# Storing the inverse row sums of a softmax from their column form

## The chip, the cores and the metric

The kernel runs on one core of a Trainium2 chip. A core has a matrix engine (TensorE, PE in the profile; its weight loads are shown apart as PEld), a vector engine (VectorE, DVE), an engine for activations (ScalarE, ACT), a general one (GpSimd, POOL) and one that issues transfers (SyncE, SP), each with an instruction queue that it works through in order. Sixteen DMA engines move data between device memory (DRAM) and the on-chip memory SBUF. TensorE writes into eight banks of an accumulation memory (PSUM). The metric is the time of one execution on the device, in microseconds (us).

## The reference

One layer of a decoder over 1024 tokens of width 1024, in float32. A combined projection gives a pooled branch (four groups of 128 channels) and eight attention heads of width 64 with a forget gate. Attention is causal, with a bias from the running sum of the gates' logarithms:

```python
s = einsum('bhqd,bhkd->bhqk', qb, k) * scale
s = s + cq[..., :, None] - cf[..., None, :]
s = where(kpos <= qpos, s, NEG_INF)
p = softmax(s, axis=-1)
out = einsum('bhqk,bhkd->bhqd', p, v)
...
x = layer_norm(ALPHA * x + concat(pool_out, attn_out) @ w_out)
x = layer_norm(ALPHA * x + square(relu(x @ w_mlp1)) @ w_mlp2)
```

The MLP's hidden width is 4096. The part in question is the division in the softmax: each of the 8 × 1024 rows of `p` has one sum, by whose inverse the row's 64 outputs are multiplied.

## The kernel before

Every float32 matrix product is done as three products of a high and a low part (`three`, L80 to L84). The stages follow one another on TensorE: the projection of values and gates, the pooled groups, attention for four pairs of heads, the output projection with the first normalization, and then the MLP's two products in a form that needs fewer multiplications (L796, L1136). All is one instruction stream; a scheduler orders each engine's queue by its own estimates, so an edit at one place can shift instructions for some distance around it.

Attention works in units: a pair of heads `p`, one head `e` of the pair, and a block `m` of 256 queries. The first three pairs run `m` from 3 down to 0, head by head; the last pair runs `m` from 0 up to 3 with both heads at each `m`. While one unit's probabilities are made, the unit before it is multiplied with its values, and pieces of other work (the next pair's query and key projection, in the last pair one pooled group and the output projection) are put in between by a credit counter (`fillstep`).

- `att_probs` (L353 to L383) makes the unit's probabilities for two rows of 128 queries. TensorE writes logits to a bank `s` (L375), DVE adds the bias and takes a minimum (L380), and ACT takes the exponential (L382), whose sum over the keys it adds up into one column of `rsum[h]`, a tile of 128 queries by 8 query rows.
- `att_values` (L385) turns the probabilities with TensorE into one of two banks named `pt` (L405), ACT and DVE copy them out as a high and a low part (L406, L407), and TensorE multiplies them with the values into a bank `pv` (L420). The two halves are added into a tile `U` (L429, L430), which SP stores to `mix_dram` (L432, L434). So the attention output is stored with the channels in partitions and the queries along the row, undivided.
- The inverses are taken by DVE in `att_values` (L443) from `rsum[h]`: for the first three pairs once a head, at `m == 0`, all eight columns; in the last pair for each unit, two columns. They stand as columns, 128 queries in the partitions. `row_scales` (L463 to L469) runs behind the unit's last multiplication: TensorE turns the columns into rows of a `pt` bank (L466), ACT copies these rows to a tile `row` (L468), and SP stores them to `rin_dram`, 8 heads by 1024 queries (L469). There are 14 such calls.
- `attention_part` (L577 to L586) reads `mix_dram` and, spread over 64 partitions for each head, the rows of `rin_dram` (L580), multiplies them on DVE (L584), and splits the product for the output projection (`out_proj`), whose weights come partly from `wo_dram` (L561).

The names in the profile's rows are those of these tiles; numbers behind a name are left out there.

Of the kernel before, what the change touches and what calls it, by code (L numbers as in the profile page):

```python
# [14 lines left out]
P = 128  # L15
S = 1024
D = 1024
NT = S // P
# [18 lines left out]
def trunk(ctx, tc, xT, xn, wuqk, wvf, bf, poolw, pscale, wout, g1, b1, w1, w2, g2, b2, out):  # L37
# [5 lines left out]
    nc = tc.nc  # L43
# [7 lines left out]
    def slot(tag, shape, dt=F32R):  # L51
        uid[0] += 1
        return sb.tile([P] + list(shape), dt, tag=tag, bufs=NBUF[tag], name=f"{tag}{uid[0]}")

    def small(shape, tag, dt=F32, bufs=1, pool=None):
        uid[0] += 1
        return (pool or sb).tile(list(shape), dt, tag=tag, bufs=bufs, name=f"{tag}_{uid[0]}")
# [5 lines left out]
    def bank(tag=None):  # L63
        uid[0] += 1
        if tag is None:
            tag = CYCLE[rr[0] % 8]
            rr[0] += 1
        return ps.tile([P, CH], F32, tag=tag, bufs=PBUF[tag], name=f"{tag}{uid[0]}")
# [18 lines left out]
    ident = small([P, P], "ident")  # L87
# [17 lines left out]
    rin_dram = dr.tile([NH, S], F32, name="rin_dram")  # L105
# [152 lines left out]
    def run(gen):  # L258
        for _ in gen:
            pass  # L260
# [124 lines left out]
    def att_values(p, e, m, prob, ahead):  # L385
        h = 2 * p + e
        rows = slice(e * HD, (e + 1) * HD)
        orow = slice((1 - e) * HD, (2 - e) * HD)
        if "values" not in fill:
            fill["values"] = bank("pv")  # L390
        ov = fill["values"][:, 256 * fill["half"] : 256 * fill["half"] + 256]
        fill["half"] = 1 - fill["half"]

        def turned(jp):
            tp = bank("pt")
            tt = slot("A", [2, CH])
            if jp < m:
                blocks = [(jj * 256 + ii * P, 2 * jp + jj, ii) for jj in range(2) for ii in range(2)]
                ev = slice(0, CH)
            else:  # L400
                blocks = [(P, 2 * jp + 1, 1), (2 * P, 2 * jp, 0), (3 * P, 2 * jp, 1)]
                ev = slice(P, CH)
                nc.gpsimd.memset(tt[:, :, 0:P].bitcast(F32), 0.0)
            for col, j, ii in blocks:
                fill["turn"] = nc.tensor.transpose(tp[:, col : col + P], prob[ii][:, j * P : (j + 1) * P], ident).ins  # L405
            nc.scalar.copy(tt[:, 0, ev], tp[:, ev])  # L406
            fill["sub"] = nc.vector.tensor_tensor(tt[:, 1, ev], tp[:, ev], tt[:, 0, ev].bitcast(F32), ALU.subtract).ins  # L407
            return tt

        def multiply(jp, tt):  # L410
            mov = ((0, 256), (256, CH)) if jp < m else ((256, CH), (0, 256))
            with ExitStack() as order:
                for behind in (fill["piece"], fill["turn"]):
                    if behind:
                        order.enter_context(tc.issue_after(behind))
                for s in range(2):
                    for jj in range(2):
                        j = 2 * jp + jj
                        a, b = mov[jj]
                        nc.tensor.matmul(  # L420
                            ov, V[j][:, h].rearrange("p s d -> p (s d)"), tt[:, s, a:b],
                            start=(j == 0 and s == 0), stop=(j == 2 * m + 1 and s == 1),
                        )
            if jp == m:
                last = p == NPAIR - 1
                if not last or e == 0:
                    fill["mx"] = slot("U", [256], F32)
                mx = fill["mx"]
                nc.scalar.copy(mx[rows], ov[orow])  # L429
                nc.vector.tensor_tensor(mx[rows], ov[rows], mx[rows], ALU.add)  # L430
                if not last:
                    nc.sync.dma_start(mix_dram[m, rows, NG + p, :], mx[rows])  # L432
                elif e:
                    nc.sync.dma_start(mix_dram[m, :, NG + p, :], mx)  # L434
                if last:
                    row_scales(h, 2 * m, 2)
                elif m == 0:
                    row_scales(h, 0, NT)

        if p == NPAIR - 1 or m == 0:  # L440
            ri = small([P, NT], "ri", bufs=3)
            i, n = (2 * m, 2) if p == NPAIR - 1 else (0, NT)
            nc.vector.reciprocal(ri[:, :n], rsum[h][:, i : i + n])  # L443
            inverse[h, i] = ri

        for jp in range(m + 1):
            left.append((multiply, jp, turned(jp)))
            if jp == 0:
                fill["last"] = fill["sub"]
                next(ahead, None)  # L450
            if jp == min(m, (m + 1) // 2 + 1):
                run(ahead)
            fillstep()
            values(2)

    left, inverse = [], {}

    def values(n):
        while len(left) > n:
            step, jp, tt = left.pop(0)  # L460
            step(jp, tt)

    def row_scales(h, i, n):  # L463
        ri = inverse.pop((h, i))
        tp = bank("pt")
        nc.tensor.transpose(tp[0:n, 0:P], ri[:, :n], ident)  # L466
        row = small([NT, P], "row")
        nc.scalar.copy(row[0:n], tp[0:n, 0:P])  # L468
        nc.sync.dma_start(rin_dram[h, i * P : (i + n) * P].rearrange("(i q) -> i q", q=P), row[0:n])  # L469

    g0 = qk_proj(0)
    for _ in range(2 * KT):
# [222 lines left out]
    def fillstep():  # L695
        fill["credit"] += fill["rate"]
        while fill["credit"] >= 1.0:
            fill["credit"] -= 1.0
            piece = next(fill["gen"], None)
            if piece and fill["pieces"] < 8:  # L700
                fill["piece"], fill["pieces"] = piece, fill["pieces"] + 1
# [4 lines left out]
    for n, unit in enumerate(order):  # L706
        p = n // 8
        if n % 8 == 0:
            if p + 1 < NPAIR:
                gen, pieces, over = qk_proj(p + 1, "mm"), 4 * KT + 1, 28  # L710
            else:
                gen, pieces, over = last_fill(), 2 * KT + 2 + 4 * KT, 27
            fill.update(gen=gen, credit=0.0, rate=pieces / over)
        prob = {}
        ahead = att_probs(*unit, prob)
        if pend is None:
            run(ahead)
        if n + 1 < len(order):
            gate_row(2 * order[n + 1][0] + order[n + 1][1])
        if pend is None:  # L720
            for g in EARLY[1:]:
                pool_linear(g, "A")
        fillstep()
        if pend is not None:
            att_values(*pend, ahead)
        pend = (*unit, prob)
        if n % 8 == 7 and n + 1 < len(order):
            run(gen)
    att_values(*pend, iter(()))
    values(0)  # L730
    run(gen)
# [603 lines left out]
```

## Time and profile before

| | |
|---|---|
| median of 3 runs | 1028.21 us (1027.87 to 1028.32) |
| the profiled execution | 1028.26 us, its span 1026.5 us |
| granted TensorE clock in it | 0.997 of full speed |
| busy: PE, PEld, DVE, ACT, POOL | 99%, 82%, 73%, 50%, 15% of the span |
| first and last reciprocal (L443) | 134.2 and 322.8 us |
| first and last transpose of inverses (L466) | 143.3 and 329.9 us |
| packets, data moved | 113399 packets, 206.17 MB |

The profile is of one execution and its times are counted from the start of the span. In a group's row stand the line, the engine, the operation and the tiles written and read, then the count, the busy time and the mean of one, and behind a bar the idle time before them with what ended most of it. In a row of the timeline the first two numbers are start and duration, and in square brackets stands the idle time before it and what ended it. Matmuls overlap, so a row's duration is longer than the distance to the next start.

### The profile page before, as it was taken

What the parts mean: (1) busy time and instruction counts of PE and PEld (TensorE: products, weight loads), DVE (VectorE), ACT (ScalarE), POOL (GpSimd) and SP (SyncE); (2) the same over time, 40 slices, a digit from 0 to 9 for tenths busy, and PEclk for the clock granted to TensorE, in tenths of its full rate; (3) what the DMA queues carried; (4) which work ended last, traced back from release to release, by engine and by line L of the source; (5) the groups of instructions that cost most, each with busy time, mean ns of one, the idle gap of its engine ahead of it and who ended that gap; (6) DMA issues with size and microseconds to landing.
All of it is one profiled execution on the core that took longest, in us unless ns stands there. A gap on an engine that the chain in (4) does not pass through costs nothing.

```text
span 1026.5 us, 14095 instructions
## 1 busy us (share of the span) xinstructions
PE 1013.1 (99%) x4976; PEld 843.8 (82%) x4976; DVE 754.4 (73%) x1303; ACT 513.3 (50%) x825; POOL 153.6 (15%) x269
## 2 busy tenths in 40 slices
PE   9999999999999999999999999999999999999996
PEld 9988888888788888888888888888888888888884
DVE  6576677777868798989888787798866565565547
ACT  5423665666755333678667667669521121221152
POOL 0200111111110032112221221220000000000057
PEclk9999999999999999999999999999999999999998
DMA  9702211111682633259676675665999888878753
GB/s 354 285 28 88 97 52 53 34 48 52 205 290 91 188 141 103 82 185 362 235 273 236 241 275 222 251 260 191 350 309 289 298 265 264 289 237 274 231 179 123
DMA packets 113399, 206.17 MB, mean 201 GB/s; under 512 B 9576, under 2 KB 77608, under 8 KB 113328
## 3 DMA queue, kind: packets, MB, share of 16 engines
q1 hardware_dynamic: 94176, 136.97, 40.7%
q0 software_dynamic: 18720, 67.64, 17.0%
q8 instruction: 39, 0.64, 0.2%
q10 hardware_dynamic: 432, 0.66, 0.2%
q14 instruction: 32, 0.26, 0.1%
HBM read 132.29 MB, written 72.94 MB: 200 GB/s over the span
## 4 chain that ended last, share of the span: by engine, by line
PE 58%; DVE 2%; issue 0%; ACT 0%; DVEq 0%
PE s L1136 17%; PE s L796 11%; PE pv L1136 9%; PE mm L796 7%; PE pt L796 7%; PE pv L796 4%; PE pt L1136 2%; PE mm L1136 2%; DVE B L71 0%; DVE bns L639 0%; DVE A L664 0%; DVE pt L661 0%; DVE pt L1153 0%; DVE A L870 0%; DVE pv L1153 0%
## 5 line engine op out<-in xcount | busy, mean ns | idle before, releaser
L71 ACT CAST B<-S 128x1024 fp32r<-128x1024 f32 (+1 forms) x78 | 67.6, 880 | 162.9 <-DMA S<-in_w_dram 85.0
L796 PE MATMUL s<-B,Q 128*128 128x512 f32 x492 | 116.4, 389 | 0.2 <-ACT B L71 0.2
L796 PEld LDWEIGHTS s<-B,Q 128*128 128x128 f32 x492 | 92.3, 188 | 19.7 <-ACT B L71 0.6
L71 DVE TENSOR_TENSOR B<-S,B 128x1024 fp32r<-128x1024 f32 (+1 forms) x78 | 78.0, 1008 | 37.7 <-ACT B L71 37.6
L1136 PE MATMUL s<-B,Q 128*128 128x512 f32 x402 | 98.5, 390 | 0.0
L1136 PEld LDWEIGHTS s<-B,Q 128*128 128x128 f32 x402 | 75.5, 188 | 16.5
L71 ACT CAST Q<-S 128x1024 fp32r<-128x1024 f32 (+2 forms) x54 | 55.7, 1031 | 63.6 <-PE s L796 17.0
L921 POOL DMA_DIRECT2D hid_dram<-A x90 | 48.1, 538 | 218.1 <-ACT A L918 171.5
L1136 PE MATMUL s<-B,A 128*128 128x512 f32 x321 | 80.3, 394 | 0.0
L71 DVE TENSOR_TENSOR Q<-S,Q 128x1024 fp32r<-128x1024 f32 (+2 forms) x54 | 65.5, 1213 | 12.8 <-ACT Q L71 12.6
L796 PE MATMUL pt<-B,Q 128*128 128x512 f32 x312 | 74.6, 389 | 0.0
L1136 PEld LDWEIGHTS s<-B,A 128*128 128x128 f32 x321 | 60.4, 188 | 13.9
L796 PE MATMUL mm<-B,Q 128*128 128x512 f32 x300 | 71.6, 389 | 0.0
L382 ACT ACTIVATE A<-A,nm 128x1024 f32<-128x1024 f32 (+7 forms) x64 | 49.7, 777 | 42.0 <-DVE nm L380 41.9
L407 DVE TENSOR_TENSOR A<-pt,A 128x512 fp32r<-128x512 f32 (+1 forms) x80 | 50.1, 633 | 25.1 <-ACT A L406 24.3
L796 PEld LDWEIGHTS pt<-B,Q 128*128 128x128 f32 x312 | 58.5, 188 | 12.1
L796 PEld LDWEIGHTS mm<-B,Q 128*128 128x128 f32 x300 | 56.3, 188 | 11.7
L919 DVE TENSOR_TENSOR A<-A,A 128x1024 f32<-128x1024 f32 x45 | 53.6, 1218 | 0.0
L406 ACT CAST A<-pt 128x512 fp32r<-128x512 f32 (+1 forms) x80 | 42.4, 541 | 22.2 <-PE pt L405 21.6
L375 PE MATMUL s<-Q,Q 128*128 128x512 f32 (+2 forms) x192 | 52.2, 368 | 1.3 <-DVE nm L380 1.3
L420 PE MATMUL pv<-A,B 128*128 128x256 f32 x320 | 53.1, 289 | 0.2 <-DVE U L430 0.2
L420 PEld LDWEIGHTS pv<-A,B 128*128 128x128 f32 x320 | 45.8, 189 | 6.4 <-DVE U L430 3.2
(432 smaller groups left out, 2290.1 us busy)
## 6 DMA issues: line engine op xcount, KB each, us to landing
hid_dram<-A POOLq DMA_DIRECT2D x105, 512.0 KB, 3.8
S<-in_w_dram SPq DMA_DIRECT2D x62, 512.0 KB, 4.4
Q<-hid_dram SPq DMA_DIRECT2D x98, 256.0 KB, 5.3
A<-hid_dram SPq DMA_DIRECT2D x82, 256.0 KB, 5.3
S<-in_wuqk_dram SPq DMA_DIRECT2D x12, 512.0 KB, 4.7
wo_dram<-Q POOLq DMA_DIRECT2D x10, 512.0 KB, 4.3
B<-wo_dram SPq DMA_DIRECT2D x10, 512.0 KB, 6.8
Q<-hid_dram SPq DMA_DIRECT2D x39, 128.0 KB, 3.2
```

The source lines that it names most:

```text
L71: return nc.scalar.copy(hi, src).ins, nc.vector.tensor_tensor(lo, src, hi.bitcast(F32), ALU.subtract).ins
L375: nc.tensor.matmul(sp, rows, KS[:, a:b], start=n == 0, stop=n == 1 and not diag)
L382: nc.scalar.activation(pt[:, :nk], pt[:, :nk], AF.Exp, bias=nm, scale=-1.0, accum_out=rsum[h][:, i : i + 1])
L406: nc.scalar.copy(tt[:, 0, ev], tp[:, ev])
L407: fill["sub"] = nc.vector.tensor_tensor(tt[:, 1, ev], tp[:, ev], tt[:, 0, ev].bitcast(F32), ALU.subtract).ins
L420: nc.tensor.matmul(ov, V[j][:, h].rearrange("p s d -> p (s d)"), tt[:, s, a:b], start=(j == 0 and s == 0), stop=(j == 2 * m + 1 and s == 1),)
L796: nc.tensor.matmul(dst, b[x][:, k], A[a][y][:, k], start=first and k == 0 and i == 0, stop=k == H - 1 and i == 2, skip_group_check=not first,)
L919: nc.vector.tensor_tensor(x, x, hi.bitcast(F32), ALU.subtract)
L921: nc.gpsimd.dma_start(hid_dram[self.u, :, i, AT[name] : AT[name] + 2 * CH], part.rearrange("p q n t -> p (q n t)"))
L1136: nc.tensor.matmul(dst, h[:, p_], w[q_], start=first and u == self.us[0] and j == 0, stop=u == self.us[-1] and j == 2, skip_group_check=no ...
```

## The change

The inverses are stored where they are made. `ri` goes from SBUF straight to `rin_dram`, one float at a time: the store's pattern takes the 128 partitions as the fast index of the row in memory and the two or eight columns as the slow one. The transpose, the copy and the store of rows are gone, and with them `row_scales` and its tile; `ri` has four buffers in place of three, as a store now reads it. The values in `rin_dram` and its readers are the same.

```diff
@@ -432,16 +432,12 @@
                     nc.sync.dma_start(mix_dram[m, rows, NG + p, :], mx[rows])
                 elif e:
                     nc.sync.dma_start(mix_dram[m, :, NG + p, :], mx)
-                if last:
-                    row_scales(h, 2 * m, 2)
-                elif m == 0:
-                    row_scales(h, 0, NT)
 
         if p == NPAIR - 1 or m == 0:
-            ri = small([P, NT], "ri", bufs=3)
             i, n = (2 * m, 2) if p == NPAIR - 1 else (0, NT)
+            ri = small([P, NT], "ri", bufs=4)
             nc.vector.reciprocal(ri[:, :n], rsum[h][:, i : i + n])
-            inverse[h, i] = ri
+            nc.sync.dma_start(rin_dram[h, i * P : (i + n) * P].rearrange("(i q) -> q i", q=P), ri[:, :n])
 
...
-    left, inverse = [], {}
+    left = []
 
...
-    def row_scales(h, i, n):
-        ri = inverse.pop((h, i))
-        tp = bank("pt")
-        nc.tensor.transpose(tp[0:n, 0:P], ri[:, :n], ident)
-        row = small([NT, P], "row")
-        nc.scalar.copy(row[0:n], tp[0:n, 0:P])
-        nc.sync.dma_start(rin_dram[h, i * P : (i + n) * P].rearrange("(i q) -> i q", q=P), row[0:n])
```

TensorE's queue is quoted where the first head's inverses were turned. `A` are the probabilities, `mm` the projection that is threaded in, `pv` the product with the values; the numbers tell the buffers apart. Before:

```order
L82 MATMUL mm_1478<-B_404,B_1475 128x512
L466 MATMUL pt_1543<-ident_63,ri_1433 8x128
L83 MATMUL mm_1478<-B_404,B_1475 128x512
L84 MATMUL mm_1478<-B_404,B_1475 128x512
L405 MATMUL pt_1548<-ident_63,A_1457 128x128
L405 MATMUL pt_1548<-ident_63,A_1444 128x128
L420 MATMUL pv_1216<-A_1436,B_417 128x256 x4
L405 MATMUL pt_1548<-ident_63,A_1457 128x128
L405 MATMUL pt_1548<-ident_63,A_1444 128x128
```

And now:

```order
L82 MATMUL mm_1479<-B_404,B_1476 128x512
L405 MATMUL pt_1544<-ident_63,A_1458 128x128
L405 MATMUL pt_1544<-ident_63,A_1445 128x128
L405 MATMUL pt_1544<-ident_63,A_1458 128x128
L405 MATMUL pt_1544<-ident_63,A_1445 128x128
L83 MATMUL mm_1479<-B_404,B_1476 128x512
L84 MATMUL mm_1479<-B_404,B_1476 128x512
L420 MATMUL pv_1216<-A_1437,B_417 128x256 x4
```

The four value transposes took the place, and the bank, of the transpose of the inverses, ahead of two projection matmuls; they are no longer parted by the four value matmuls.

The second place is SP's queue at the begin of the last pair, where loads of the output weights (`wo_dram`) are issued. Before:

```order
L561 DMA B_3065<-wo_dram 128x1024
L561 DMA B_3066<-wo_dram 128x1024
L432 DMA mix_dram<-U_3041 64x256
L561 DMA B_3215<-wo_dram 128x1024
L469 DMA rin_dram<-row_3120 8x128
L561 DMA B_3216<-wo_dram 128x1024
L432 DMA mix_dram<-U_3114 64x256
```

And now:

```order
L549 DMA B_3047<-wo_dram 128x1024
L440 DMA rin_dram<-ri_2986 128x2x1
L440 DMA rin_dram<-ri_3060 128x2x1
L549 DMA B_3048<-wo_dram 128x1024
L432 DMA mix_dram<-U_3023 64x256
L549 DMA B_3184<-wo_dram 128x1024
L549 DMA B_3185<-wo_dram 128x1024
L432 DMA mix_dram<-U_3097 64x256
L440 DMA rin_dram<-ri_3104 128x2x1
```

The store of a head's eight columns moved up out of this stretch, and the last pair's first two stores came in between the first load and the second. All lines behind the edit count 4 or 12 fewer than before (the reads of `rin_dram` are L568, the loads of `wo_dram` L549).

## The prediction

> **What bounds the kernel now.** I read the page first, then the busy time by stage, then the stage of the change by tile, by wait and row by row. The page:
>
> ```profile
> PE 1013.1 (99%) x4976; PEld 843.8 (82%) x4976; DVE 754.4 (73%) x1303; ACT 513.3 (50%) x825; POOL 153.6 (15%) x269
> PE   9999999999999999999999999999999999999996
> PEclk9999999999999999999999999999999999999998
> PE 58%; DVE 2%; issue 0%; ACT 0%; DVEq 0%
> ```
>
> TensorE is busy in every slice at its full clock, and the chain that ended last lies on it. The busy share alone could hide stalls, so the stages (columns: stage, its length, busy time and instructions of PE, PEld, DVE, ACT, POOL, clock, share of the DMA engines, GB/s):
>
> ```profile
> 125.00:345.00 220.00, 217.84 (x1270) 181.17 (x1269) 164.99 (x395) 137.76 (x295) 33.11 (x85) 1.00 0.34 107
> 275.00:300.00 25.00, 24.73 (x143) 20.22 (x142) 16.87 (x43) 15.79 (x38) 3.50 (x7) 1.00 0.88 295
> 345.00:1026.00 681.00, 671.55 (x2969) 552.07 (x2967) 508.17 (x735) 319.94 (x433) 110.90 (x144) 1.00 0.68 236
> ```
>
> The change lies in 125 to 345 us, attention and the work threaded through it. There DVE is busy for 165 and ACT for 138 of 220 us: TensorE is the bound, but it takes part in chains with both. After 345 us come the MLP's matmuls, 2969 of them in 681 us, 0.23 us each; that stage follows whatever time TensorE comes out of attention, so a microsecond saved on TensorE's queue before 345 should arrive at the end as one. In 275 to 300 us the DMA engines are 88% busy, which matters below for the stores.
>
> **What is removed.** Fourteen of each (six with eight columns, eight with two), from the views by tile of `ri` and of `row` (minimum, median, maximum in ns; first and last start):
>
> ```profile
> L443 DVE RECIPROCAL ri<-rsum x14: 154/166/203, 134.2 to 322.8; 128x2 f32<-128x2 f32 x8, 128x8 f32<-128x8 f32 x6
> L466 PE MATMUL pt<-ident,ri x14: 270/272/275, 143.3 to 329.9; 128*2 128x128 f32 x8, 128*8 128x128 f32 x6
> L468 ACT COPY row<-pt x14: 237/254/255, 143.6 to 330.3; 2x128 f32<-2x128 f32 x8, 8x128 f32<-8x128 f32 x6
> L469 SPq DMA_DIRECT2D rin_dram<-row x14: 244/264/295, 143.9 to 330.6; - x14
> ```
>
> The reciprocals stay. The transpose's 272 ns is latency, not what it costs the queue, for matmuls overlap. The timeline of TensorE around the first one (start, duration) shows the queue's cost:
>
> ```profile
> 142.85 0.40 PE L84 MATMUL mm<-B,B 128*128 128x512 f32 x1
> 143.08 0.40 PE L82 MATMUL mm<-B,B 128*128 128x512 f32 x1
> 143.31 0.27 PE L466 MATMUL pt<-ident,ri 128*8 128x128 f32 x1
> 143.34 0.47 PE L83 MATMUL mm<-B,B 128*128 128x512 f32 x1
> 143.66 0.40 PE L84 MATMUL mm<-B,B 128*128 128x512 f32 x1
> ```
>
> Undisturbed, one 512-column matmul starts 0.23 us after the other (142.85, 143.08). From 143.08 to 143.66 stand two such steps, 0.46 us, and the transpose: 0.58 − 0.46 = 0.12 us. Fourteen of them: 14 × 0.12 = 1.7 us of TensorE's queue, surely gone.
>
> Then the waits. `row` is copied out of a `pt` bank, of which there are two, and the value transposes (L405) use the same two. They wait for the copy (us in total, times), and the transpose itself waits for the bank:
>
> ```profile
>   PEld pt L405: 2.3, 6
>   PE pt L405: 0.3, 1
> PEld pt L466 <- DVE A L407: 1.4, 6, 0.2
> ```
>
> One such wait in the row-by-row view:
>
> ```profile
> 275.47 0.33 PE L375 MATMUL s<-Q,Q 128*128 128x384 f32 x1
> 276.07 0.66 PE L405 MATMUL pt<-ident,A 128*128 128x128 f32 x4 [0.27 <-ACT row L468]
> 276.48 0.42 PE L375 MATMUL s<-Q,Q 128*128 128x384 f32 x1
> 276.75 0.23 PE L377 MATMUL s<-maskb,identb 128*128 128x128 bf16 x1
> ```
>
> The 384-column matmul at 275.47 holds the queue 0.60 us to the next start; its twin at 276.48 needs 0.27. So 0.33 us are really lost at this place. Weight loads run ahead of the matmuls by about one load, which is why 2.3 us of waiting there is not 2.3 us of TensorE: I take off one load of 0.19 us (188 ns in the page's groups, row below) per wait, 2.3 − 6 × 0.19 = 1.2 us, the 0.3 us being part of it. Bounds of this term: 0.3 us (what the matmul queue itself shows as idle) and 2.6 us (both rows in full). The 1.4 us before L466 I count as nothing: the next transposes ask for the same bank, freed by the same DVE subtraction, so that wait passes to them; at most 1.4 − 6 × 0.19 = 0.3 us.
>
> ```profile
> L796 PEld LDWEIGHTS s<-B,Q 128*128 128x128 f32 x492 | 92.3, 188 | 19.7 <-ACT B L71 0.6
> ```
>
> ACT loses 14 × 0.254 = 3.6 us of 138. It is not the bound, and I count zero; but ACT is in order, and what follows the copy there is the exponential of the next unit, for which transposes wait:
>
> ```profile
> PEld s L375 <- DVE nm L380: 4.2, 9, 0.9
> PEld pv L420 <- DVE U L430: 3.2, 10, 0.6
> PEld pt L405 <- ACT A L382: 2.2, 8, 0.4
> ```
>
> The third row, 2.2 us, is the upper bound of a gain there. The first two are the stalls that the change doesn't touch and that could swallow what it saves.
>
> **What is added and moved.** No instruction is new on TensorE, DVE or ACT. The fourth `ri` buffer costs nothing in time: a reciprocal waits only for a store four units back. New is the store's shape: 128 × 8 or 128 × 2 single floats 4 bytes each, set down 512 bytes apart along a partition's elements, instead of 8 or 2 rows of 512 bytes. Nothing in the trace is stored like this, so I bound it. Issuing: a row store takes 0.26 us on SP's queue, a broadcast read of `rin_dram` with more pieces 0.60 us (median):
>
> ```profile
> L580 SPq DMA_DIRECT2D S<-rin_dram x10: 477/597/654, 281.3 to 350.3; - x10
> ```
>
> If issuing grew with the pieces, the 1024 pieces of an early store would hold SP for some microseconds, but SP has room there: around the first store it issues a load and the store 2.2 us apart and sits in between,
>
> ```profile
> 141.71 0.33 SPq L75 DMA_DIRECT2D S<-in_wuqk_dram  x1
> 143.90 0.29 SPq L469 DMA_DIRECT2D rin_dram<-row  x1
> ```
>
> and no wait of TensorE for a DMA stands in the list of waits of this stage. Transfer: between 309 and 312 us there are 378 packets, nearly all of 1 KB, on one queue:
>
> ```profile
> q1 hardware_dynamic: 378, 0.36, 48.4%
> ```
>
> 48.4% of 16 × 3 us is 23.2 us, 61 ns a packet. A 4-byte packet costs between nothing and this; an early store then is 64 packets on each engine, 0 to 3.9 us, a late one 16, 0 to 1.0 us. I take the low end, as 4 bytes are far below 1 KB, and keep the high one for the slow rival.
>
> The place on SP: the store now stands behind the reciprocal instead of behind the row's copy, so what is queued behind it waits for DVE. The tightest spot is where two late stores stand between two loads of `wo_dram`:
>
> ```profile
> 269.18 0.16 DVE L443 RECIPROCAL ri<-rsum 128x2 f32<-128x2 f32 x1
> 272.55 0.17 DVE L443 RECIPROCAL ri<-rsum 128x2 f32<-128x2 f32 x1
> 267.28 1.56 SPq L561 DMA_DIRECT2D B<-wo_dram  x2
> 273.10 0.53 SPq L561 DMA_DIRECT2D B<-wo_dram  x1
> 284.81 2.31 SPq L561 DMA_DIRECT2D B<-wo_dram  x5
> B<-wo_dram SPq DMA_DIRECT2D x10, 512.0 KB, 6.8
> 281.94 0.39 PE L82 MATMUL mm<-B,Q 128*128 128x512 f32 x1
> 295.85 0.41 PE L82 MATMUL mm<-B,Q 128*128 128x512 f32 x1
> ```
>
> The second load of the first row, issued by 268.8 before, now waits for the reciprocal at 272.55: 4 us late, landing near 272.55 + 6.8 = 279.4. Its matmuls are the fourth triple of the output projection, which begins at 281.94, so not before 281.94 + 9 × 0.23 = 284.0: covered by 4.6 us; without that cover the 4 us would be TensorE's. The last five loads land by 287.1 + 6.8 = 293.9; the attention half's first matmul that can need them starts at 295.85. Cover: 2 us.
>
> **Sum.** −1.7 (slots) − 1.2 (bank waits) + 0 (ACT, SP, DMA) = −2.9 us against the profiled execution's 1028.26 (span 1026.5, 1.8 outside it, untouched): 1025.4. The median of the runs, 1028.21, is 0.05 beside it, so the same number stands. Its own range, by the bounds of the bank term and the 0.3: −1.7 − 0.3 to −1.7 − 2.6 − 0.3, that is 1023.7 to 1026.3. The finishing parts after attention (the reads of `mix_dram` and `rin_dram`, the multiplication, the split) move with TensorE or have room.
>
> **Rivals.**
>
> *The waits move on.* The matmul slots saved are spent waiting for DVE: 4.2 and 3.2 us already stand there, and the new order puts transposes directly behind one another where L466 and two matmuls stood between. For it: these waits have nothing to do with `row`. Against it: there is matmul work to fill in from the projection. Half of the slots' 1.7 us survives: about 1027.4.
>
> *More than the sum.* Exponentials come earlier by the copy that stood before them, and the 2.2 us on ACT goes too, with the bank waits in full: 1.7 + 2.6 + 2.2 = 6.5, 1021.8. For it: the copy stands directly before L382 at the first place. Against it: ACT is idle a third of this stage.
>
> *Slower, by the single-float stores.* They share the queue with the `wo_dram` loads where DMA is 88% busy. One early store and four late ones fall between 261 and 293 us: 64 + 4 × 16 = 128 packets an engine. At 61 ns these are 7.8 us; less 2 us cover, TensorE waits 5.8 us, less the 2.9 saved: +2.9, 1031.2. It turns slower above (2 + 2.9) / 128 = 38 ns a packet.
>
> The Trainium skill speaks for this rival: "DMA: Bandwidth & Descriptors", section "Rules for kernel authors", says that a strided last dimension becomes one descriptor per element and is to be rearranged instead. The same page's "Specifications" has it that below 512 bytes the engine reads, modifies and writes. No run here shows such a store; by these rules the cost is nearer the high end, the 1031.2 above, by the trace's small packets I hold it unlikely.
>
> **How the numbers follow.** A measurement of this kernel tells no change from one of 0.2%, 2.06 us: faster is below 1026.15. Forecast 0.45, nearly all of it faster (0.38 and 0.07 within); waits move on 0.22 (0.21 within, 0.01 faster); more than the sum 0.20, faster; slower by the stores or by an order that is worse by chance, 0.13 (0.12 slower, 0.01 within). Faster 0.59, same 0.29, slower 0.12. The range, 1021.0 to 1029.0, takes in the first three cases and their spread and leaves out the slow end.
>
> **What would show it.** Right: the group L466 and waits for `row` gone; in 125 to 345 us the same matmuls in some 3 us less; the MLP stage as long as before. Wrong: L405 waiting longer for ACT or DVE than the 2.2 us here; a wait of TensorE for a DMA of `B`; landing of the stores above the 6.8 us of a `wo_dram` load; or SP standing at a store while loads behind it come late.

## The result, and the profile after

The changed kernel takes 1043.68 us (median of 4 runs, 1041.50 to 1044.27) against 1028.26 us of the kernel before in the same comparison (4 runs, 1027.87 to 1030.22): ratio 1.0142, 95% interval 1.0122 to 1.0162. It is slower by 15.4 us, where 2.9 us less were forecast; the time lies outside the predicted range. The profiled execution took 1043.23 us with a span of 1041.5 us.

The page of the changed kernel, its busy times, its 40 slices of TensorE and of the clock, and its count of DMA packets:

```profile
PE 1016.5 (98%) x4962; PEld 847.0 (81%) x4962; DVE 755.2 (73%) x1303; ACT 511.8 (49%) x811; POOL 153.7 (15%) x269
...
PE   9999999999798999999999999999999999999996
...
PEclk9999999999989999999999999999999999999999
...
DMA packets 121687, 206.17 MB, mean 198 GB/s; under 512 B 17928, under 2 KB 85896, under 8 KB 121616
```

TensorE has 14 instructions fewer, as it should, and ACT too. But the row of slices that was all nines (but for the last) has a 7 and an 8 between 260 and 340 us, and the clock has an 8. The busy times by stage (stage, its length, busy time and instructions of PE, PEld, DVE, ACT and POOL, clock, DMA share, GB/s):

```profile
125.00:150.00 25.00, 23.31 (x138) 19.48 (x136) 17.57 (x42) 14.79 (x32) 3.81 (x10) 1.00 0.22 54
...
275.00:300.00 25.00, 18.90 (x83) 14.94 (x83) 13.10 (x31) 12.83 (x28) 3.74 (x7) 0.80 0.89 169
300.00:345.00 45.00, 40.97 (x231) 33.91 (x231) 28.93 (x69) 22.29 (x40) 3.12 (x7) 0.96 0.80 174
360.00:1041.00 681.00, 671.32 (x2972) 552.63 (x2970) 508.46 (x735) 321.27 (x435) 110.71 (x144) 1.00 0.68 236
```

The last row is the MLP stage: 681 us with 671.32 us of TensorE, as before (671.55), only it starts 15 us later. The whole loss lies ahead of it. From 275 to 300 us TensorE was busy for 24.73 us with 143 matmuls before; now it is busy for 18.90 us with 83, and the clock is 0.80. DMA is as busy there as before (0.89 against 0.88) but moves 169 GB/s in place of 295.

Who waited, in 125 to 360 us (total in us, times, longest):

```profile
PEld pv L420 <- DVE U L430: 9.4, 13, 3.5
ACT Q L71 <- DMA S<-mix_dram: 9.1, 2, 6.9
ACT U L429 <- DMA mix_dram<-U: 7.0, 3, 4.6
...
PE pv L420 <- DVE U L430: 5.0, 3, 3.1
...
PE mm L82 <- DVE B L609: 3.9, 1, 3.9
```

The first, third and fourth kind are one chain: ScalarE waits for the `mix_dram` store of an older `U` buffer, its copy comes late, VectorE's sum comes late, and the value matmuls on TensorE wait. The second kind is ScalarE waiting for loads of `mix_dram` (0.8 us in all before the change). The last, TensorE's longest single wait, begins at a load too, as the rows further down show. The first place, row by row (start, duration, engine, what; in brackets the idle time before it and its releaser):

```profile
133.62 0.37 SPq L440 DMA_DIRECT2D rin_dram<-ri  x1
...
134.37 0.46 SPq L432 DMA_DIRECT2D mix_dram<-U  x1
...
145.33 0.39 PE L84 MATMUL mm<-B,B 128*128 128x512 f32 x1
146.53 0.37 ACT L429 COPY U<-pv 64x256 f32<-64x256 f32 x1 [2.20 <-DMA mix_dram<-U]
146.94 0.42 DVE L430 TENSOR_TENSOR U<-pv,U 64x256 f32<-64x256 f32 x1 [1.87 <-ACT U L429]
147.41 1.21 PE L420 MATMUL pv<-A,B 128*128 128x256 f32 x8 [1.69 <-DVE U L430]
```

The single-float store of `ri` is issued at 133.62, and the `mix_dram` store right behind it at 134.37. ScalarE gets that store's buffer back only at 146.5, 12 us later, and TensorE starts nothing from 145.33 to 147.41. The view of the tile `ri` has the same 12 us as the time from issue to landing, and shows that SP's issue of such a store is short (ns, minimum, median, maximum):

```profile
L440 SPq DMA_DIRECT2D rin_dram<-ri x14: 360/377/932, 133.6 to 338.9; - x14
...
DMA to landing us min/median/max: 10.0/12.1/14.5
```

TensorE has three longer stalls behind 270 us, and two of them begin at loads that come late, not at a `mix_dram` store:

```profile
275.51 1.04 ACT L71 CAST B<-S 128x1024 fp32r<-128x1024 f32 x1 [4.59 <-DMA S<-in_wout_dram]
...
278.33 1.09 PE L420 MATMUL pv<-A,B 128*128 128x256 f32 x4 [3.10 <-DVE U L430]
...
285.10 0.36 ACT L429 COPY U<-pv 64x256 f32<-64x256 f32 x1 [4.61 <-DMA mix_dram<-U]
...
286.35 0.90 PE L405 MATMUL pt<-ident,A 128*128 128x128 f32 x3 [3.00 <-ACT A L382]
...
321.62 1.28 DVE L609 SCALAR_TENSOR_TENSOR B<-B,mm 128x512 f32<-128x512 f32 x2 [4.36 <-DMA B<-in_xn_dram]
...
322.37 0.50 PE L82 MATMUL mm<-B,Q 128*128 128x512 f32 x1 [3.90 <-DVE B L609]
```

At 278 us ScalarE had waited for a load of the output weights (`in_wout_dram`, issued from 267.0 us, 8.5 and 8.9 us to landing, 3.5 us before the change), and its copy of `U` stood behind that. At 286 us it had waited for a `mix_dram` store. At 322 us VectorE had waited for a load of `x` (`in_xn_dram`), issued at 312.87 us right behind a single-float store at 312.46, and landed 8.8 us later.

### The profile page after: what moved, and what is told of

The parts are those of the page before. It is cut to its first block, busy times and chain, and to the rows that moved or that the text cites. A ratio compares the mean times of both kernels' runs of the same rounds, so it can differ in the third digit from the quotient of the medians.

```text
span 1041.5 us, 14054 instructions
## 1 busy us (share of the span) xinstructions
PE 1016.5 (98%) x4962; PEld 847.0 (81%) x4962; DVE 755.2 (73%) x1303; ACT 511.8 (49%) x811; POOL 153.7 (15%) x269
## 4 chain that ended last, share of the span: by engine, by line
PE 57%; DVE 2%; issue 0%; ACT 0%; DVEq 0%
PE s L1124 17%; PE s L784 10%; PE pv L1124 8%; PE mm L784 7%; PE pt L784 7%; PE pv L784 4%; PE pt L1124 2%; PE mm L1124 2%; DVE B L71 0%; DVE bns L627 0%; DVE A L652 0%; DVE pt L649 0%; DVE pt L1141 0%; DVE A L858 0%; DVE pv L1141 0%
## 5 line engine op out<-in xcount | busy, mean ns | idle before, releaser
L407 DVE TENSOR_TENSOR A<-pt,A 128x512 fp32r<-128x512 f32 (+1 forms) x80 | 50.4, 633 | 26.4 <-ACT A L406 25.6
```

## The experiments

The theories at the start. **A**: many 4-byte pieces are slow to be written and hold up what is behind them, either on their own queue alone (**A1**) or on every queue (**A2**). **B**: the stores' earlier place on SP's queue and the new order on TensorE lose the time. All times are medians, each with the kernel before on the same chip.

| run | us | before | ratio, 95% interval |
|---|---|---|---|
| e1_contig | 1030.25 | 1028.44 | 1.0018 (1.0007 to 1.0028) |
| e2_aside | 1071.01 | 1028.44 | 1.0412 (1.0390 to 1.0435) |
| e3_act | 1074.31 | 1028.44 | 1.0448 (1.0430 to 1.0465) |
| e4_pool | 1067.16 | 1028.44 | 1.0378 (1.0363 to 1.0394) |
| e5_blocks | 1026.19 | 1028.41 | 0.9979 (0.9970 to 0.9987) |
| e6_contig_behind | 1030.47 | 1028.41 | 1.0018 (1.0007 to 1.0030) |
| e7_early | 1041.95 | 1028.41 | 1.0130 (1.0117 to 1.0143) |
| e8_late | 1044.81 | 1028.41 | 1.0162 (1.0148 to 1.0177) |
| e9_price (one run) | 1053.36 | 1028.44 | |
| e10_pairmix | 1048.66 | 1028.44 | 1.0209 (1.0180 to 1.0238) |
| e11_blocks_pairmix | 1027.12 | 1028.44 | 0.9985 (0.9976 to 0.9994) |
| e12_bank | 1027.54 | 1028.44 | 0.9991 (0.9982 to 1.0000) |
| e13_price2 (one run) | 1033.23 | 1028.16 | |
| e14_spread | 1028.44 | 1028.16 | 0.9999 (0.9990 to 1.0009) |

### The pattern of the store alone: e1_contig

```diff
-nc.sync.dma_start(rin_dram[h, i*P : (i+n)*P].rearrange("(i q) -> q i", q=P), ri[:, :n])
+nc.sync.dma_start(rin_dram[h, i*P : (i+n)*P].rearrange("(q i) -> q i", i=n), ri[:, :n])
```

> The changed kernel, whose stores set the same floats down next to one another in memory: 128 pieces of 32 or 8 bytes in place of 1024 or 256 pieces of 4 bytes. The inverses land in permuted places, so the attention output is scaled by the wrong rows; instructions, their order on TensorE and the waits are those of the changed kernel. Theory A (the many 4-byte pieces are slow to be written and hold up what is queued behind them): the loss goes with the pieces and the gain that was predicted appears, 1024 to 1028 us. Theory B (the store's earlier place on SyncE's queue and the new order on TensorE lose the time): nothing of that is changed, 1043 us.

It took 1030.25 us: 13.4 of the 15.4 us are gone with nothing but the pattern of the store, so for these A's forecast came and B's didn't. 1.8 us above before stayed, and the foretold gain of 2.9 us was not there. The view of `ri` before and after 268 us, that is the six stores of 32-byte pieces and the eight of 8-byte pieces (us to landing, minimum, median, maximum):

```profile
L440 SPq DMA_DIRECT2D rin_dram<-ri x6: 320/326/327, 134.3 to 261.4; - x6
...
DMA to landing us min/median/max: 1.4/1.4/1.6
...
L440 SPq DMA_DIRECT2D rin_dram<-ri x8: 319/355/503, 269.6 to 326.2; - x8
...
DMA to landing us min/median/max: 4.6/5.2/8.0
```

Both kinds have 128 pieces, and the smaller ones take longer; but the eight also fall into the stretch where DMA was 88% busy before, so this doesn't show that their size is the reason. One wait of ScalarE for a `mix_dram` store was left, 4.2 us at 277 us, and TensorE started nothing for 3.6 us there.

### The single floats alone, and on other queues: e2_aside, e3_act, e4_pool

```diff
 # e2_aside: the kernel before, behind the reciprocal
+nc.sync.dma_start(aside_dram[h, i*P : (i+n)*P].rearrange("(i q) -> q i", q=P), ri[:, :n])
 # e3_act and e4_pool: the changed kernel
-nc.sync.dma_start(rin_dram[...], ri[:, :n])
+nc.scalar.dma_start(rin_dram[...], ri[:, :n])      # e3_act
+nc.gpsimd.dma_start(rin_dram[...], ri[:, :n])      # e4_pool
```

> The kernel before, with transposes, copies and row stores, to which the fourteen stores of single floats are added, into a tensor that nobody reads. Theory A: the added stores alone lose what the change lost and the removed work does not come back, so 1028 + 15 + up to 3: 1040 to 1048 us. Theory B: the stores move nothing that matters, TensorE's order is all but the one before, 1028 to 1030 us.

> The changed kernel with its fourteen stores issued by ScalarE, so on another DMA queue than the loads and the stores of the attention output; fourteen issues of some 0.4 us come onto ScalarE. Theory A1 (the pieces hold only the queue they stand in): most of the loss goes, 1026 to 1031 us. Theory A2 (the pieces hold the DMA engines or the memory for every queue): 1038 to 1045 us. Theory B: SyncE's queue is as before the change again, 1026 to 1031 us.

> The changed kernel with its stores issued by GpSimd, on its own software queue; TensorE's order is that of the changed kernel. GpSimd stands in the chain of the logits (it adds the mask and clears the transposed tiles), so that time it spends on making descriptors can delay these. Theory A1: 1026 to 1032 us. Theory A2: 1038 to 1045 us. Theory B, as far as SyncE's place loses the time: 1026 to 1031 us; as far as TensorE's order does: 1043 us.

The signs are A's, and A2's for the two other queues, but the sizes were missed by far: 43, 46 and 39 us lost where at most 20 were expected. Putting the stores on another queue makes them worse. Two rows of the waits show where it goes, of e2_aside:

```profile
ACT row L470 <- DMA rin_dram<-row: 25.9, 4, 11.3
...
ACT U L430 <- DMA mix_dram<-U: 11.4, 5, 4.2
```

and of e3_act:

```profile
PE pv L420 <- DVE U L430: 27.7, 8, 9.1
ACT U L429 <- DMA mix_dram<-U: 23.3, 5, 11.2
```

In e2_aside the row-form stores stand behind the single floats too, and `row` has one buffer, so ScalarE waits for it as well. In e3_act the `mix_dram` stores are on SP's queue, the single floats on ScalarE's, and ScalarE still waits for the former, up to 11.2 us at once. Why they come later than with all stores on one queue is not settled by these runs.

### Blocks in place of pieces, and the place on SP: e5_blocks, e6_contig_behind

```diff
 # e5_blocks, from the changed kernel
-ri = small([P, NT], "ri", bufs=4)
+ri, rt = small([P, 32], "ri", bufs=2), small([P, 32], "rt32", bufs=4)
+nc.gpsimd.memset(ri, 0.0)
 nc.vector.reciprocal(ri[:, :n], rsum[h][:, i : i + n])
-nc.sync.dma_start(rin_dram[...], ri[:, :n])
+nc.vector.transpose(rt, ri)
+for b in range(4):
+    nc.sync.dma_start(rin_dram[h, i*P : (i+n)*P].rearrange("(i b q) -> b i q", b=4, q=32)[b], rt[32*b : 32*b + n])
 # e6_contig_behind: the store of e1_contig, issued behind the mix_dram store of its group
```

> The inverses are turned by VectorE in blocks of 32x32 (the column tile is widened to 32 columns, the other 24 or 30 of them zeros), and each store becomes four, one for each block, of 8 or 2 pieces of 128 bytes: 32 or 8 pieces a head in place of 1024 or 256. The stores stand at the changed kernel's place on SP's queue, and TensorE has no turn of them and no bank. Theory A (what costs is the number of small pieces; the 1.8 us that 128 pieces of 32 or 8 bytes still lost is the same thing, smaller): 1023 to 1027 us, the foretold gain appears, and no ScalarE wait for a mix_dram store above 2 us. Theory B (those 1.8 us come from the earlier place on SP's queue, ahead of the mix_dram store): 1029 to 1032 us, with the wait of about 4 us for a mix_dram store at 277 us still there.

> 128 pieces of 32 or 8 bytes a store, as in the run with 128 pieces before (the inverses lie permuted in rin_dram, so that rows are scaled by other rows' inverses), but each store is issued where the rows were stored before the change, behind the mix_dram store of its group. TensorE's order is that of the changed kernel. Theory A (number of pieces): 1029 to 1032 us as with the store ahead. Theory B (place on SP's queue): 1024 to 1027 us, and the wait for a mix_dram store at 277 us is gone.

e6_contig_behind moves the stores back to where they stood before the change and takes 1030.47 us (single runs 1026.68 to 1034.92), the same as e1_contig: no price of the place on SP's queue shows. e5_blocks leaves them at the new place and takes 1026.19 us, 2.2 us less than the kernel before. So B is out, also for the 1.8 us that e1_contig had left. In e5_blocks ScalarE waits 0.2 us for `in_wout_dram`, and nothing waits for the load of `in_xn_dram` into `B`: these loads, too, came late only with the single floats. TensorE has no stall in e5_blocks where the changed kernel had its worst:

```profile
275.00:300.00 25.00, 25.00 (x145) 21.05 (x145) 16.74 (x48) 14.40 (x32) 3.98 (x11) 1.00 0.87 310
```

e5_blocks computes the same outputs and is the fastest kernel of this study, though it issues 56 stores in place of 14 and gives VectorE 14 more instructions of 0.21 us.

### Which of the stores: e7_early, e8_late

```diff
+to = floats if n == NT else contiguous       # e7_early; e8_late the other way round
-nc.sync.dma_start(rin_dram[...].rearrange("(i q) -> q i", q=P), ri[:, :n])
+nc.sync.dma_start(to, ri[:, :n])
```

> Only the six early stores keep single floats (6 x 1024 pieces); the eight of the last pair are 128 pieces of 8 bytes, permuted, so that the first 1024 rows of the last pair's heads are scaled by other rows' inverses. If the price goes by the number of pieces, three quarters of the 13.4 us are here: 1039 to 1042 us. If it goes by the place (the last pair's stores come between 270 and 340 us, where the mix_dram stores and their U buffers follow close behind): 1032 to 1036 us, with the stall at 145 us and one near 275 us left.

> Only the eight stores of the last pair keep single floats (8 x 256 pieces); the six early ones are 128 pieces of 32 bytes, permuted, so that the rows of the other six heads are scaled by other rows' inverses. By the number of pieces, a quarter of the 13.4 us: 1032 to 1035 us. By the place: 1036 to 1041 us, with the stalls near 283 and 318 us still there and none at 145 us.

Each half alone loses as much as both together: 13.5 and 16.4 us against 15.4. e7_early is where the number of pieces put it, e8_late is above both expectations, and the two add up to twice the whole: the loss isn't a sum over pieces or over stores. First e7_early, then e8_late:

```profile
125.00:150.00 25.00, 21.28 (x127) 17.90 (x125) 16.43 (x38) 14.19 (x31) 3.40 (x10) 0.99 0.24 51
275.00:300.00 25.00, 19.84 (x99) 15.14 (x98) 14.30 (x38) 12.77 (x32) 3.39 (x7) 0.86 0.62 179
```

```profile
125.00:150.00 25.00, 25.00 (x152) 21.35 (x151) 18.89 (x46) 16.57 (x36) 4.03 (x11) 1.00 0.19 54
275.00:300.00 25.00, 17.38 (x89) 14.31 (x87) 8.35 (x24) 9.86 (x22) 2.94 (x5) 0.86 0.88 125
```

Without early single floats the stall at 145 us is gone in e8_late. In e7_early it is larger (TensorE busy 21.28 of 25 us) than in the changed kernel (23.31), although the same stores are issued up to there. How much of a store's landing becomes a stall thus changes from one traced execution to the next by more than the stores do; each kernel has one trace, and what sets it is open.

### The store by itself: e9_price

```diff
 # e5_blocks, one more store behind those of each early head, k = 0 to 5
+aside_dram[k] <- ri[:, :8], [:, :4], [:, :2], [:, :1]  as single floats, "(i q) -> q i"
+aside_dram[k] <- ri[:, :8], ri[:, :32]                 as one piece a partition, "(q i) -> q i"
```

> Built on the run with blocks of 32x32. Behind each of the six early heads' stores one more store goes from the column tile ri to a tensor that is never read: in order of time 128x8, 128x4, 128x2 and 128x1 single floats 512 bytes apart, then 128 pieces of 32 bytes and 128 pieces of 128 bytes. Theory A (the time to landing goes by the number of pieces): about 10 to 14 us, 6 to 7, 4 to 5, 2 to 4, and the two last 2 to 4 us each; the whole near 1028 to 1032 us. Rival (it goes by the size of a piece, below 512 bytes always slow): all six above 8 us, and the whole above 1035 us.

GpSimd clears the next `ri` buffer as soon as the store before has landed, so its row gives the landing. On GpSimd, and then the issue of the same stores on SP, for the 1st, 4th and 5th of the six:

```profile
147.17 0.12 POOL L440 MEMSET ri<- 128x32 f32 x1 [13.01 <-DMA aside_dram<-ri]
...
243.02 0.12 POOL L440 MEMSET ri<- 128x32 f32 x1 [12.09 <-DMA aside_dram<-ri]
264.83 0.13 POOL L440 MEMSET ri<- 128x32 f32 x1 [2.45 <-DMA aside_dram<-ri]
```

```profile
134.04 0.37 SPq L451 DMA_DIRECT2D aside_dram<-ri  x1
...
232.15 0.33 SPq L451 DMA_DIRECT2D aside_dram<-ri  x1
...
263.32 0.33 SPq L454 DMA_DIRECT2D aside_dram<-ri  x1
```

From issue to landing: 13.1 us for 1024 single floats and 10.9 us for 128 of them, but 1.5 us for 128 pieces of 32 bytes. Each is one store in one execution. The others: 11.6 us for 512 floats, 9.5 for 256, and 1.8 us for 128 pieces of 128 bytes. Theory A as it stood, that the number of pieces counts, falls: an eighth of the pieces takes nearly as long. The rival, that all below 512 bytes is slow, falls too. (The 1053 us of the whole are no price: the clearing of `ri` made GpSimd wait 53 us in all, and the inverses behind it.)

### Size of a piece, or its neighbours: e13_price2, e14_spread

Two theories were left. **S**: a piece of 4 bytes is slow by its size. **L**: neighbouring floats of one store fall into the same 64 bytes and are written one after the other; putting them apart would make them fast.

```diff
 # e13_price2: the six extra stores of e9_price with other patterns
+c floats a partition, z floats from one to the next: (c, z) = (1, 1), (1, 16), (1, 128), (8, 16)
+one piece of 2 floats, one of 4 floats a partition, next to each other
 # e14_spread, from e2_aside: the tensor gets a last axis of 128 floats, of which one is written
-aside_dram[h, i*P : (i+n)*P].rearrange("(i q) -> q i", q=P)
+aside_dram[h, i*P : (i+n)*P, 0].rearrange("(i q) -> q i", q=P)
```

> Six stores from the column tile to a tensor that is never read, behind the stores in blocks of the six early heads, in order of time: 128 single floats next to each other, 128 floats 64 bytes apart, 128 floats 512 bytes apart, 1024 floats 64 bytes apart, 128 pieces of 8 bytes next to each other, 128 pieces of 16 bytes next to each other. Theory S (a piece of 4 bytes is slow by its size): 10 to 13 us to landing for the first four, 5 us or more for 8 bytes. Theory L (pieces that fall into the same 64 bytes are written one after the other, some 0.65 us each: 16 floats about 10.5 us): 10 to 11 us for the first, 1.5 to 3 us for the next two, 2 to 4 us for the 1024, 5 to 6 us for 8 bytes, 2.5 to 3.5 us for 16 bytes.

> The kernel before with the 14 extra single-float stores to a tensor that is never read, as in the run that cost 42.6 us, with the same order on every engine and the same number of pieces; but the floats lie 512 bytes apart in that tensor in place of next to each other. Theory S (size of the piece): 1060 to 1075 us, as with neighbouring floats. Theory L (same 64 bytes): 1028 to 1034 us.

e13_price2, landing on GpSimd and then issue on SP, for 128 floats next to each other, 128 floats 64 bytes apart, and 1024 floats 64 bytes apart:

```profile
142.97 0.12 POOL L440 MEMSET ri<- 128x32 f32 x1 [8.91 <-DMA aside_dram<-ri]
167.64 0.34 POOL L440 MEMSET ri<- 128x32 f32 x1 [1.61 <-DMA aside_dram<-ri]
...
220.25 0.28 POOL L440 MEMSET ri<- 128x32 f32 x1 [4.82 <-DMA aside_dram<-ri]
```

```profile
133.98 0.32 SPq L455 DMA_DIRECT2D aside_dram<-ri  x1
166.00 0.32 SPq L455 DMA_DIRECT2D aside_dram<-ri  x1
...
216.65 0.58 SPq L455 DMA_DIRECT2D aside_dram<-ri  x1
```

The same 128 floats take 9.0 us next to each other and 1.6 us put 64 bytes apart (1.8 us at 512 bytes); 1024 floats put apart take 3.6 us, where 1024 with neighbours took 13.1. Adjacent pieces of 16 bytes took 2.5 us. Those of 8 bytes landed within 3.4 us, less than the 5 to 6 us that L gave, so the price falls with the number of neighbours, but not in proportion to it. These too are single stores.

e14_spread decides it for the whole kernel. It has the order of e2_aside on TensorE, VectorE, ScalarE and SP, and the same 14 stores of the same 8192 floats. Landing in e2_aside, and then in e14_spread (us, minimum, median, maximum), from the views by tile of `aside_dram`:

```profile
DMA to landing us min/median/max: 10.1/11.1/12.2
```

```profile
DMA to landing us min/median/max: 1.6/2.6/6.2
```

The time falls from 1071.01 us to 1028.44 us, no difference from the kernel before. Not the number of pieces and not their 4 bytes cost the time, but that neighbouring floats were written side by side. That they are written one after the other in units of 64 bytes is an inference: 64 bytes is the smallest distance tried, and the unit may be smaller.

### The way to TensorE: e10_pairmix, e11_blocks_pairmix

```diff
-if not last or e == 0:
+at = e if last else (m + 1) % 2
+if at == 0:
     fill["mx"] = slot("U", [256], F32)
-copy, sum and mix_dram store on mx[rows]
+copy, sum and mix_dram store on the half "at" of mx
```

> The changed kernel with its single-float stores, but two successive 64-row mix_dram stores of the first three pairs come from the two halves of one U buffer, so that a half becomes free three or four groups later in place of two (the last pair's stores stay). Theory A2 with the U buffer as the way by which the slow stores reach TensorE: 1035 to 1040 us, no ScalarE wait for a mix_dram store before 270 us. Rival (the slow stores hold loads too, so another wait takes its place): 1041 to 1045 us.

> The blocks of 32x32 with the paired U buffers. As ScalarE waited nowhere above 2 us for a mix_dram store in the run with blocks, all theories expect no change from its 1026.2 us: 1025 to 1027.5. It is the control to the paired buffers with single floats.

The stages of e10_pairmix:

```profile
125.00:150.00 25.00, 25.00 (x152) 21.14 (x151) 18.43 (x44) 16.39 (x35) 4.07 (x11) 1.00 0.23 52
...
275.00:300.00 25.00, 12.45 (x47) 9.86 (x46) 7.81 (x20) 9.45 (x21) 4.06 (x7) 0.73 0.88 140
```

At first it went as expected: TensorE is busy for 25.00 us of 125 to 150 us, where the changed kernel had 23.31, and no wait for a `mix_dram` store is left there. So the stall at 145 us did go through the `U` buffer. Behind 275 us, where the last pair's stores stand and the buffers are as before, TensorE lost more than ever (busy for 12.45 of 25 us from 275 to 300), and the whole took 1048.66 us (1045.01 to 1055.55), missing both expectations. The trace is that of the slowest of the six runs. Buffers that come free later move the stall; they don't cure the store. e11_blocks_pairmix, 1027.12 us, is within the interval of e5_blocks: by themselves the paired buffers bring nothing.

### The bank wait by itself: e12_bank

```diff
-tp = bank("pt")
+tp = bank("s")      # the kernel before, in row_scales
```

> The kernel before, with the turn of the inverses in a bank of s (three of them) in place of pt (two). If the bank wait that the prediction put at 1.2 us is on TensorE's path: 1026.8 to 1027.6 us. If the wait is made up for elsewhere: 1028.0 to 1028.8. If the matmuls that need s (the scores) now wait for it: 1029 to 1031.

1027.54 us, 0.9 us less than before, with an interval from no gain to 1.9 us. The wait of L405 for the copy of `row` (2.3 us before) is gone, and in its place L405 waits longer for ScalarE's exponential (3.6 us against 2.2) and VectorE (2.1 against 0.7). The term of 1.2 us that the prediction gave to this wait fits the interval, which reaches down to no gain at all.

## Why the prediction was wrong

**The gain was there.** In e5_blocks, which removes the same transposes, copies and bank waits, the kernel gains 2.2 us (interval 1.3 to 3.1) where the sum said 2.9. The sum is thus about right, with some of it spent in waits for VectorE, as the first rival said: L405 waits 2.2 us for L407 there in place of 0.7. Of its terms only the bank waits (1.2) were measured by themselves, 0.9 us in e12_bank; the slots (1.7) were not. "More than the sum" did not come.

**The place on SP, the issue and the `wo_dram` cover held.** e1_contig against e6_contig_behind shows no price of the place. SP's issue of a single-float store took 0.377 us (median), nothing that would hold the queue. The `wo_dram` loads took longer to land (median 8.7 us in place of 6.8), but no engine waited for them.

**The step that failed** is the price of the single-float stores: "A 4-byte packet costs between nothing and this", "I take the low end, as 4 bytes are far below 1 KB". It priced a store by the time of its packets on the engines, and bounded that by the 61 ns a packet of transfers that were nearly all of 1 KB. What sets the loss is the time until the writes have landed: 10.0 to 14.5 us with neighbouring floats, against 1.6 to 6.2 us with the same packets put apart. No row of the trace before holds that time, and packets an engine was the wrong unit: between 137 and 140 us the changed kernel's trace has no packet at all, while the `mix_dram` store issued right behind the first single-float store lands only at 146.5 us. Even the high end of the bound, 3.9 us a store, was a third of the truth.

**What the step named as delayed was right only in part.** It looked at the `wo_dram` loads behind the stores, with 4.6 and 2 us of cover. The first things hit are the 64-KB `mix_dram` stores, which come right behind, because a `U` buffer is needed again two groups later. Other loads were hit as well: the stalls at 278 and 322 us begin at `in_wout_dram` and `in_xn_dram`, for which the sum had no term. Of the list of what would show it wrong, three came: the landing above 6.8 us, L405 waiting for ScalarE's exponential longer than 2.2 us (6.6 us), and TensorE waiting, by way of VectorE, for a load into `B`. A wait of ScalarE for the store of a tile that it had written was not in it.

**The rival "slower by the single-float stores"** (chance 0.13, 1031.2 us) had the sign, but its mechanism, the engines' time per packet with a turning point of 38 ns, is refuted by e14_spread: the same packets cost nothing. It counted four late stores between 261 and 293 us, where the trace before has five late reciprocals (the fifth at 290.81 us, behind the last of the loads). The rules that were weighed beside it, from the Trainium skill, "DMA: Bandwidth & Descriptors", pointed the right way for this store. But one descriptor (the order to move one piece) per element ("Rules for kernel authors") was harmless in e14_spread, and so was a size below 512 bytes ("Specifications") in the 1.5 to 1.8 us of 128 pieces of 32 or 128 bytes and of 128 floats put apart. What hurt, floats beside each other, is in neither rule.

**Still open**: why the same slow stores cost 15 us in the changed kernel, 13 to 16 in either half of it, and 39 to 46 when they are extra or on another queue. The waits show by which buffers the delay comes in, not why it grows.

## What to carry to other kernels

A store in single floats is to be priced by its time to landing and by what stands behind it on the queue, with the buffers that wait for that, not by its bytes or packets. Where a column is to be stored as a row, turn it in blocks first, so that each piece is 128 bytes: here 32 × 32 blocks on VectorE gave what the change was worth (1026.19 us against 1028.41), while single floats beside each other lost 15 us. An engine that waits for the store of a tile it wrote earlier is a sign that something ahead of that store on the queue lands late.

## What the hardware showed that was not expected

- The landing of neighbouring single floats hardly depends on their number: 9.0 and 10.9 us for 128, 13.1 us for 1024. Put 64 bytes apart, 128 take 1.6 us and 1024 take 3.6 us.
- Behind slow stores on one queue, stores on another come late too: with the single floats on ScalarE's queue, `mix_dram` stores on SP's were waited for 23.3 us in all, with those on SP's own queue 7.0 us.
- A stall of TensorE of 3.4 to 4.2 us, from one start to the next, costs more than itself: behind it the clock falls for some 3 to 6 us. Of the changed kernel, TensorE idle and then slow (columns as in the stages above):

```profile
318.00:322.00 4.00, 0.47 (x4) 0.20 (x2) 0.38 (x1) 0.97 (x3) 0.00 (x0) 1.00 0.82 47
322.00:326.00 4.00, 3.63 (x10) 2.84 (x11) 3.99 (x11) 0.12 (x1) 0.00 (x0) 0.61 0.83 276
```

  With 0.47 us of work from 318 to 322 us, the clock granted in the next 4 us is 0.61. In rows of one microsecond it is 0.50 from 279 to 281, 286 to 292 and 323 to 326 us. The Trainium skill, "TensorE: Matmul & The Clock Gate", Part 1, says that about 3.4 us without work bring the array to half its clock; these rows agree. The shorter stall, 2.08 us at 145 us, left the clock at 1.00. An estimate of the whole loss from these numbers: the four stalls (2.08, 3.50, 3.38 and 4.24 us from start to start, less 0.23 us each) take 12 us, and some 12 us at half the clock lose 6; less the 2.2 us that e5_blocks gained, that is 16 us, close to the 15.4 us of the change.
